# Low halves of the second product's activations on VectorE, and another order of its seven partial products

## The chip, the cores and the metric

The kernel runs on one core of a Trainium2 chip. The metric is device time in microseconds (us) for one execution; a median of several runs stands for a kernel. The engines of the core work side by side, each through its own queue in order: TensorE (PE in the profile; its weight loads are PEld), VectorE (DVE), ScalarE (ACT), GpSimd (POOL) and SyncE (SP), which here only issues transfers. They wait for each other by semaphores.

## The reference

One layer of a decoder: a combined input projection, two mixers (a gated recurrence and a short convolution), an output projection, and a dense MLP with a squared ReLU, each followed by a layer norm. There are 2048 prompt tokens and 64 sample tokens; the model width is 1024, the MLP's inner width 4096, all in float32.

```python
    mix = jnp.einsum('btm,md->btd', jnp.concatenate([o.astype(x.dtype), yc], axis=-1), w_out)
    x = _layer_norm(ALPHA * x + mix, ln1_g, ln1_b)

    hid = jnp.square(jax.nn.relu(jnp.einsum('btd,df->btf', x, w_ff1)))
    x = _layer_norm(ALPHA * x + jnp.einsum('btf,fd->btd', hid, w_ff2), ln2_g, ln2_b)
```

The change lies in the product of `hid` with `w_ff2`.

## The kernel before

The prompt is cut into four blocks (`b` = 0 to 3) of 512 tokens. Each block goes through the mixers and the output projection (`main` and the loops behind it), the MLP's first product (`ff1`) and its second (the loop over `pl["ff2"]`). The 64 sample tokens go with block 1 (`samp`).

**Three matmuls for one.** A float32 operand is split into a high part that TensorE takes in its fp32r form and a low part, the rest. `mm3_on` (L234 to L238) makes high x high (L236), high x low weights (L237) and low x high weights (L238). `h` and `l` are the parts of the activations, `wh` and `wl` of the weights. A high part is a copy on ScalarE, a low part a subtraction.

**Weights.** A weight unit is 128 x 1024 values. `unit_dma` (L173) has SyncE load it into one of three buffers `st`; `unit_split` makes `wh` on ScalarE (L194) and `wl` on VectorE (L201), four buffers each. `weights(u)` keeps this up to three units ahead of the matmuls. The subtraction isn't issued at once: it goes to the list `later`, and `flush` issues what the list holds at the start of the next `weights` call. `split` (L154 to L156) is the same for any tile: a copy on ScalarE at once, the subtraction on VectorE by way of `later`.

**Seven products for eight.** The second product is done in eight chunks `c` of 512 inner values, each as a 2 x 2 block product in seven multiplications. The activations of a chunk are the tile `raw[c]` with four slots (two halves of the inner values times two halves of the tokens). The weights are quarters (`B11`, `B21`, `B12`, `B22`) or sums of quarters (`T1` to `T4`), which GpSimd's accumulating transfers write to DRAM during block 0 (`make_sums`, called from block 0's `main` loop). `PRODUCTS` sets the order of the seven steps and the pair of PSUM banks (`A` to `D`) into which a step adds; inside a step all chunks follow each other. `INTO` says where a step's banks are added to the output rows once its last chunk is done: `add_to`, on VectorE (L1069, L1072), reads the bank from PSUM, first the bank of the first 128 tokens (its six matmuls come first), then the other. Steps of one letter go on adding into the same banks. The last chunk of block 3 is done in plain form at the very end (`pl["last"]`), and its activations are split during the last step.

**Activations of a step.** `prepare` runs two units ahead of the matmuls. It copies slot `SLOT_OF[step]` of `raw[c]` to `h` on ScalarE (L1040) and has GpSimd subtract to get `l` (L1041). Three of the seven steps need a sum of slots that isn't in `raw` yet: after `T4`, `T2` and `T1` were prepared, a subtraction on VectorE writes the next one (L1045, L1047, L1049), by way of `later`, eight in each of these steps. One more sum is made while `ff1` runs (`chunk_done`, L990).

**Sample rows, block 1.** Four steps (`SAMPLE`) also multiply the sample tokens, both parts in one tile `hp` (`sample_rows`, `mm_pair`, L241 and L242): four matmuls after the unit's twelve. At the step's end `sample_sums` copies half of the bank to SBUF on ScalarE (`upper`, L247) and adds twice on VectorE for each half of the output that the step goes into (L1080 or L1083, then L1084): two operations for `B21`, `T1` and `B22`, four for `B11`.

**Next block's input.** `X_PLACES` says behind which units of the second product the next block's input tiles (`X`) are loaded and split, as units of their own in the same queue.

The lines that set the order:

```python
PRODUCTS = (("B21", "C"), ("B11", "A"), ("T4", "D"), ("T2", "A"), ("T1", "B"), ("B22", "B"), ("T3", "A"))
INTO = {"C": {"B21": ((2, 0, 1),)}, "D": {"T4": ((0, 0, 1),)},
        "A": {"B11": ((2, 0, 1),), "T2": ((2, 1, -1),), "T3": ((0, 1, -1), (0, 0, 1))},
        "B": {"T1": ((0, 1, -1),), "B22": ((2, 1, -1),)}}
```

Of the kernel before, what the change touches and what calls it, by code (L numbers as in the profile page):

```python
# [9 lines left out]
F32 = mybir.dt.float32  # L10
F32R = mybir.dt.float32r
U8 = mybir.dt.uint8
AF = mybir.ActivationFunctionType
ALU = mybir.AluOpType
# [3 lines left out]
D = 1024  # L18
# [17 lines left out]
RAW = {"B11": 0, "B21": 1, "B12": 2, "B22": 3}  # L36
SUMS = ("T1", "T2", "T3", "T4")

PRODUCTS = (("B21", "C"), ("B11", "A"), ("T4", "D"), ("T2", "A"), ("T1", "B"), ("B22", "B"), ("T3", "A"))

SLOT_OF = {"B21": 3, "B11": 1, "T4": 2, "T2": 2, "T1": 1, "B22": 3, "T3": 0}

# [3 lines left out]

SAMPLE = {"B21": (1, ((0, 1),)), "B11": (0, ((0, 1), (1, -1))), "T1": (0, ((1, 1),)), "B22": (1, ((1, 1),))}

X_PLACES = (("B21", 2), ("B21", 5), ("B11", 2), ("B11", 5), ("B22", 5))
M_ORDER = (4, 5, 6, 7, 0, 1, 2, 3)  # L50


# [1 line left out]
def hybrid_step(ctx, tc, a, o):  # L54
# [89 lines left out]
    later = []  # L144
# [9 lines left out]
    def split(hi, lo, src):  # L154
        s.activation(hi, src, AF.Copy)  # L155
        later.append(lambda: v.tensor_tensor(lo, src, hi.bitcast(F32), ALU.subtract))  # L156
# [5 lines left out]
    def add_unit(src, scale=None, cols=D, use=None, spare=False):  # L162
        units.append((src, scale, cols, use, spare))
        return len(units) - 1
# [12 lines left out]
    def unit_split():  # L177
        i = at["split"]
        at["split"] += 1
        _, scale, _, use, spare = units[i]  # L180
        st = stages.pop(i)
        if use is not None:
            use(st)
            return
        wh = new((P, D), "wh", 4, F32R)
        if i == 0:
            wl = new((P, D), "wl", 4, F32R)
            for half in (slice(0, D // 2), slice(D // 2, D)):
                split(wh[:, half], wl[:, half], st[:, half])
                flush()  # L190
            handles[i] = (wh, wl)
            return
        if scale is None:
            s.activation(wh, st, AF.Copy)  # L194
        else:
            s.activation(wh, st, AF.Identity, scale=scale)

        def low():
            wl = TOK(F32R) if spare else new((P, D), "wl", 4, F32R)
            if scale is None:  # L200
                v.tensor_tensor(wl, st, wh.bitcast(F32), ALU.subtract)  # L201
            else:
                v.scalar_tensor_tensor(wl, st, scale, wh.bitcast(F32), ALU.mult, ALU.subtract)
            handles[i] = (wh, wl)

        later.append(low)
# [10 lines left out]
    def weights(i, kept=0):  # L217

        ahead(i + 4 - kept)
        return handles.pop(i)  # L220
# [111 lines left out]
                yield  # L332

    making = make_sums()

    for b in range(NB):
        pl = {}
# [16 lines left out]
        nx = x_units(b + 1) if b + 1 < NB else []  # L354
        for step, _ in PRODUCTS:
            for c in range(pl["nc"]):
                pl["ff2"].append((step, c, add_unit(a["w_ff2"][c * 4 + RAW[step]] if step in RAW else sums[c][step])))
                if (step, c) in X_PLACES and nx:
                    src, cols, use = nx.pop(0)
                    add_unit(src, cols=cols, use=use)  # L360
# [11 lines left out]
    for b in range(NB):  # L372
# [451 lines left out]

        for i, _ in enumerate(main()):
            rec_step()
            if b == 0 and i >= 4:
                next(making, 0)
                next(making, 0)
            if i >= 16 and i % (3 if samp else 4) == 0:  # L830
                rec_step()
            if i % 2 == 0:
                pump()
# [199 lines left out]
        def prepare():  # L1033
            if not queue:
                return
            step, c = queue.pop(0)
            r = raw[c]
            x = r[:, SLOT_OF[step]]
            h, l = F((P, 2, 256), "h", 3, F32R), F((P, 2, 256), "l", 3, F32R)
            s.activation(h, x, AF.Copy)  # L1040
            g.tensor_tensor(l, x, h.bitcast(F32), ALU.subtract)  # L1041
            hid[step, c] = (h, l)

            if step == "T4":
                later.append(lambda: v.scalar_tensor_tensor(x, r[:, 0], -1.0, x, ALU.mult, ALU.subtract))  # L1045
            elif step == "T2":
                later.append(lambda: v.scalar_tensor_tensor(r[:, 1], x, -1.0, r[:, 1], ALU.mult, ALU.subtract))  # L1047
            elif step == "T1":
                later.append(lambda: v.scalar_tensor_tensor(r[:, 3], r[:, 2], -1.0, r[:, 3], ALU.mult, ALU.subtract))  # L1049
            elif step == "T3":  # L1050
                del raw[c]

        for i, (f, u) in enumerate(pl["ff1"]):
            if i >= len(pl["ff1"]) - 2:
                prepare()
            ff1(f, weights(u), segs)
        drain()
        norm_weights(1)
        if b == 0:
            for _ in making:  # L1060
                pass

        touched = set()

# [31 lines left out]
        to = dict(PRODUCTS)  # L1096
        banks = {}
        sample_rows()
        for step, c, u in pl["ff2"]:
            w = weights(u)  # L1100
            parts = [tuple(x[:, q * 512:q * 512 + 512] for x in w) for q in range(2)]
            prepare()
            if step in SAMPLE:
                sample_rows()
            if step == "T3" and pl["last"] and 2 <= c < 6:
                if c == 2:
                    last = [F((P, 4, 2, 256), "raw", NCH, F32R) for _ in range(2)]
                split(last[0][:, c - 2], last[1][:, c - 2], raw[NCH - 1][:, c - 2])
# [159 lines left out]
```

## Time and profile before

| what | value |
|---|---|
| median of 3 runs | 2449.08 us (2446.64 to 2449.68) |
| profiled execution, its own time | 2449.19 us |
| its span, first to last instruction | 2447.4 us |
| granted TensorE clock, mean | 0.996 |
| GpSimd, `l` (L1041) | 217 instructions, 391.6 us busy |
| VectorE, `wl` (L201) | 514 instructions, 679.5 us busy, 1325 ns mean |
| ScalarE, `h` (L1040) | 217 instructions, 133.5 us busy |

In a row of waits, "PE ps L238 <- POOL l L1041: 2.2, 4, 0.9" says that TensorE's instruction of L238, which writes `ps`, was idle 2.2 us in all, four times, 0.9 at the longest, until GpSimd's instruction of L1041 had written `l`. In the order of time a row gives start, duration, engine, line, operation, `out<-in`, size and, in brackets, the idle time before it and what ended it. Matmuls are pipelined, so their durations overlap. A row of windows gives the stretch, its length, and for PE, PEld, DVE, ACT and POOL the busy time with the number of instructions, then clock, share of the DMA engines and GB/s. A group's row ends in busy time, mean ns of one, idle time before and what ended it.

### The profile page before, as it was taken

To read this page: it belongs to the slowest core of one execution; us is meant where nothing else is said; L and a number is where in the kernel's file an instruction comes from. 1 tells how busy PE (TensorE), PEld (TensorE's weight loads), DVE (VectorE), ACT (ScalarE), POOL (GpSimd) and SP (SyncE) were. 2 spreads that over 40 slices of the span, in tenths; PEclk is the share of its full clock that TensorE was granted. 3 is DMA by queue.
4 is the path that set the end of the run, shared out by engine and by line. 5 is a ranking of instruction groups with operands and counts; after the bars stand their busy time and mean duration, and the time that the engine had idled before them with its cause. 6 is when DMAs were issued, how large, how long until landed. Compare 5 with 4: busy or idle time off the path is not lost. (4 is left out here: it accounts for less than half of the span.)

```text
span 2447.4 us, 32997 instructions
## 1 busy us (share of the span) xinstructions
PE 2400.3 (98%) x12876; PEld 2051.5 (84%) x12876; DVE 1542.2 (63%) x2153; ACT 1114.9 (46%) x1794; POOL 524.9 (21%) x376
## 2 busy tenths in 40 slices
PE   7999999999999999999999999999999999999998
PEld 5888988878889889998778888988878888988876
DVE  5756822696865684227968857623886865822597
ACT  4334534654324354445554244534654334543553
POOL 3210000654001110004750000001662001000554
PEclk9999999999999999999999999999999999999999
DMA  9985423655223633225543225423654324433453
GB/s 329 277 233 174 160 97 112 199 186 179 79 78 75 211 121 104 87 96 164 180 149 118 91 80 190 144 96 129 206 188 146 104 82 159 161 103 116 163 184 113
DMA packets 103548, 358.79 MB, mean 147 GB/s; under 512 B 11552, under 2 KB 16032, under 8 KB 103392
## 3 DMA queue, kind: packets, MB, share of 16 engines
q1 hardware_dynamic: 91216, 313.88, 38.6%
q0 software_dynamic: 12032, 42.54, 6.5%
q8 instruction: 101, 1.65, 0.3%
q14 instruction: 55, 0.45, 0.1%
q10 hardware_dynamic: 144, 0.26, 0.0%
HBM read 345.59 MB, written 44.60 MB: 159 GB/s over the span
## 5 line engine op out<-in xcount | busy, mean ns | idle before, releaser
L201 DVE TENSOR_TENSOR wl<-st,wh 128x1024 fp32r<-128x1024 f32 x514 | 679.5, 1325 | 548.3 <-ACT wh L194 547.5
L230 PE MATMUL ps<-X,wh 128*128 128x512 f32 (+2 forms) x2272 | 779.6, 343 | 14.2 <-ACT X L155 11.0
L232 PE MATMUL ps<-X,wl 128*128 128x512 f32 (+2 forms) x2272 | 769.4, 339 | 1.0 <-DVE wl L201 1.0
L231 PE MATMUL ps<-X,wh 128*128 128x512 f32 (+2 forms) x2272 | 769.4, 339 | 0.5 <-DVE X L156 0.5
L194 ACT ACTIVATE wh<-st 128x1024 fp32r<-128x1024 f32 x515 | 543.1, 1055 | 381.0 <-DMA st<-T 90.8
L1041 POOL TENSOR_TENSOR l<-raw,h 128x512 fp32r<-128x512 f32 x217 | 391.6, 1808 | 947.3 <-ACT h L1040 930.9
L230 PEld LDWEIGHTS ps<-X,wh 128*128 128x128 f32 x2272 | 431.6, 190 | 60.6 <-ACT X L155 13.0
L232 PEld LDWEIGHTS ps<-X,wl 128*128 128x128 f32 x2272 | 431.3, 190 | 43.7 <-DVE wl L201 1.9
L231 PEld LDWEIGHTS ps<-X,wh 128*128 128x128 f32 x2272 | 431.7, 190 | 42.1 <-DVE X L156 2.6
L238 PE MATMUL ps<-wh,l 128*128 128x512 f32 x868 | 342.1, 394 | 8.9 <-POOL l L1041 8.9
L236 PE MATMUL ps<-wh,h 128*128 128x512 f32 x868 | 339.1, 391 | 6.3 <-DVE tok L1072 5.0
L237 PE MATMUL ps<-wl,h 128*128 128x512 f32 x868 | 339.2, 391 | 1.6 <-DVE wl L201 1.6
L1008 ACT ACTIVATE raw<-ps 128x256 f32<-128x256 f32 (+1 forms) x184 | 85.7, 466 | 372.6 <-PE ps L232 370.9
L238 PEld LDWEIGHTS ps<-wh,l 128*128 128x128 f32 x868 | 163.3, 188 | 53.1 <-POOL l L1041 19.9
L236 PEld LDWEIGHTS ps<-wh,h 128*128 128x128 f32 x868 | 163.4, 188 | 40.7 <-issue 6.2
L237 PEld LDWEIGHTS ps<-wl,h 128*128 128x128 f32 x868 | 163.2, 188 | 37.4 <-DVE wl L201 3.3
L1040 ACT ACTIVATE h<-raw 128x512 fp32r<-128x512 f32 x217 | 133.5, 615 | 7.7 <-PE ps L237 5.7
L262 POOL TENSOR_TENSOR sm<-sm,nhalf 128x1 f32<-128x1 f32 (+1 forms) x34 | 36.5, 1075 | 383.4 <-DVE sm L261 383.4
L230 PE MATMUL ps<-wh,X 128*128 128x512 f32 x256 | 104.0, 406 | 0.0
L230 PE MATMUL ps<-wh,S 128*128 128x512 f32 x256 | 101.3, 396 | 0.0
L232 PE MATMUL ps<-wh,X 128*128 128x512 f32 x256 | 100.3, 392 | 0.0
L232 PE MATMUL ps<-wh,S 128*128 128x512 f32 x256 | 99.9, 390 | 0.0
(204 smaller groups left out, 2560.4 us busy)
## 6 DMA issues: line engine op xcount, KB each, us to landing
st<-in_w_ff SPq DMA_DIRECT2D x249, 512.0 KB, 3.3
st<-T SPq DMA_DIRECT2D x124, 512.0 KB, 3.3
st<-in_w_in SPq DMA_DIRECT2D x110, 512.0 KB, 3.3
st<-in_w_out SPq DMA_DIRECT2D x56, 512.0 KB, 4.3
T<-in_w_ff POOLq DMA_DIRECT2D x48, 512.0 KB, 19.7
T<-T POOLq DMA_DIRECT2D x16, 512.0 KB, 17.8
lnb<-in_lnb SPq DMA_DIRECT2D x16, 512.0 KB, 5.9
tok<-in_x SPq DMA_DIRECT2D x16, 512.0 KB, 6.9
```

Of the source, the lines that this page charges most:

```text
L194: s.activation(wh, st, AF.Copy)
L201: v.tensor_tensor(wl, st, wh.bitcast(F32), ALU.subtract)
L230: te.matmul(out, lh, rh, start=first, stop=False)
L231: te.matmul(out, lh, rl, start=False, stop=False)
L232: te.matmul(out, ll, rh, start=False, stop=last)
L236: te.matmul(out, lh, rh, start=first, stop=False, skip_group_check=True)
L237: te.matmul(out, lh, rl, start=False, stop=False, skip_group_check=True)
L238: te.matmul(out, ll, rh, start=False, stop=last, skip_group_check=True)
L262: g.tensor_tensor(st[:n, 15:16], st[:n, 14:15], nhalf[:n, 0:1], ALU.pow)
L1008: s.activation(r[:, h0:h1], ps[:, :256 * (h1 - h0)].rearrange("p (s t) -> p s t", t=256), AF.Relu)
L1040: s.activation(h, x, AF.Copy)
L1041: g.tensor_tensor(l, x, h.bitcast(F32), ALU.subtract)
```

## The change

`l` is now made by `split`: the subtraction goes to VectorE, by way of `later`. `PRODUCTS` has another order: `T4`, `B11`, `B21`, `T2`, `T1`, `T3`, `B22`. The three kinds of sums are no longer tied to `prepare`: `sum_rows` puts one into `later` every one and a half units, number s (from 0) at unit (3s + 6) // 2, so that 24 of them (21 in block 3) lie in the first five steps. The input tiles of the next block are loaded in the last two steps instead of the first two (and one in the sixth). `make_sums` is stepped from the ninth part of `main` instead of the fifth, and its rest, if any, is issued ahead of the first product's main loop. Where the last chunk is split moves with the last step, to `B22`.

```diff
-PRODUCTS = (("B21", "C"), ("B11", "A"), ("T4", "D"), ("T2", "A"), ("T1", "B"), ("B22", "B"), ("T3", "A"))
+PRODUCTS = (("T4", "D"), ("B11", "A"), ("B21", "C"), ("T2", "A"), ("T1", "B"), ("T3", "A"), ("B22", "B"))
...
-X_PLACES = (("B21", 2), ("B21", 5), ("B11", 2), ("B11", 5), ("B22", 5))
+X_PLACES = (("T3", 0), ("T3", 4), ("B22", 0), ("B22", 3), ("B22", 5))
...
-            if b == 0 and i >= 4:
+            if b == 0 and i >= 8:
                 next(making, 0)
                 next(making, 0)
...
-            s.activation(h, x, AF.Copy)
-            g.tensor_tensor(l, x, h.bitcast(F32), ALU.subtract)
+            split(h, l, x)
             hid[step, c] = (h, l)
-
-            if step == "T4":
-                later.append(lambda: v.scalar_tensor_tensor(x, r[:, 0], -1.0, x, ALU.mult, ALU.subtract))
-            elif step == "T2":
-                later.append(lambda: v.scalar_tensor_tensor(r[:, 1], x, -1.0, r[:, 1], ALU.mult, ALU.subtract))
-            elif step == "T1":
-                later.append(lambda: v.scalar_tensor_tensor(r[:, 3], r[:, 2], -1.0, r[:, 3], ALU.mult, ALU.subtract))
-            elif step == "T3":
+            if step in ("T2", "T1", "B22"):
+                assert (step, c) in summed
+            seen.add((step, c))
+            if step == "B22":
                 del raw[c]
 
+
+        sumq = [(k, c) for k in ("T2", "T1", "B22") for c in range(ncs)]
+        summed, seen = set(), set()
+
+        def sum_rows():
+            if not sumq:
+                return
+            k, c = sumq.pop(0)
+            assert (dict(T2="T4", T1="B11", B22="B21")[k], c) in seen
+            summed.add((k, c))
+            r = raw[c]
+            to, of, less = {"T2": (2, 0, 2), "T1": (1, 2, 1), "B22": (3, 2, 3)}[k]
+            later.append(lambda: v.scalar_tensor_tensor(r[:, to], r[:, of], -1.0, r[:, less], ALU.mult, ALU.subtract))
+
+        if b == 0:
+            for _ in making:
+                pass
         for i, (f, u) in enumerate(pl["ff1"]):
...
         drain()
         norm_weights(1)
-        if b == 0:
-            for _ in making:
-                pass
...
-        for step, c, u in pl["ff2"]:
+        for n_, (step, c, u) in enumerate(pl["ff2"]):
             w = weights(u)
+            while (len(summed) * 3 + 6) // 2 <= n_ and sumq:
+                sum_rows()
             parts = [tuple(x[:, q * 512:q * 512 + 512] for x in w) for q in range(2)]
             prepare()
...
-            if step == "T3" and pl["last"] and 2 <= c < 6:
+            if step == "B22" and pl["last"] and 2 <= c < 6:
```

What this does to the queues is shown at three places. VectorE in block 0, at the end of a step behind which a sum stands: `T4` before the change (the two `tok` rows are its adds from the banks).

```order
L201 TENSOR_TENSOR wl_4087<-st_4067,wh_4069 128x1024
L1047 SCALAR_TENSOR_TENSOR raw_2149<-raw_2149 128x512
L1072 SCALAR_TENSOR_TENSOR tok_1776<-tok_1776,ps_3935 128x512
L1072 SCALAR_TENSOR_TENSOR tok_1778<-tok_1778,ps_3936 128x512
L201 TENSOR_TENSOR wl_4112<-st_4090,wh_4092 128x1024
L1047 SCALAR_TENSOR_TENSOR raw_2311<-raw_2311 128x512
```

The same engine with the change, at the end of `B11` in block 0.

```order
L1084 SCALAR_TENSOR_TENSOR tok_1929<-tok_1929,ps_3736 128x512
L1084 SCALAR_TENSOR_TENSOR tok_1931<-tok_1931,ps_3737 128x512
L201 TENSOR_TENSOR wl_3910<-st_3889,wh_3891 128x1024
L1063 SCALAR_TENSOR_TENSOR raw_2149<-raw_2149 128x512
L156 TENSOR_TENSOR l_3894<-raw_2311,h_3893 128x512
L201 TENSOR_TENSOR wl_3935<-st_3914,wh_3916 128x1024
```

Before, no `l` stood in this queue; now each unit has one, behind the unit's `wl` and sum, and all three behind the adds.

TensorE in block 0, where `T1` ends, before: its last three matmuls and the first three of `B22` (`ps_4309` and `ps_4310` are the pair B).

```order
L236 MATMUL ps_4310<-wh_4397,h_4422 128x512
L237 MATMUL ps_4310<-wl_4415,h_4422 128x512
L238 MATMUL ps_4310<-wh_4397,l_4423 128x512
L236 MATMUL ps_4309<-wh_4420,h_4445 128x512
L237 MATMUL ps_4309<-wl_4438,h_4445 128x512
L238 MATMUL ps_4309<-wh_4420,l_4446 128x512
```

With the change `T3` follows, into the pair A (`ps_3736` and `ps_3737`; B is `ps_4290` and `ps_4291`).

```order
L236 MATMUL ps_4291<-wh_4377,h_4402 128x512
L237 MATMUL ps_4291<-wl_4394,h_4402 128x512
L238 MATMUL ps_4291<-wh_4377,l_4403 128x512
L236 MATMUL ps_3736<-wh_4400,h_4428 128x512
L237 MATMUL ps_3736<-wl_4417,h_4428 128x512
L238 MATMUL ps_3736<-wh_4400,l_4429 128x512
```

The bank that VectorE has to read at the end of `T1` was written again by the next matmul, and is now left alone for a step.

VectorE in block 1, between two steps that both have sample rows. Before, from `B21` to `B11` (`tok_7428` holds the sample rows, `ps_9836` their bank):

```order
L1072 SCALAR_TENSOR_TENSOR tok_7424<-tok_7424,ps_9822 128x512
L1072 SCALAR_TENSOR_TENSOR tok_7426<-tok_7426,ps_9823 128x512
L1083 SCALAR_TENSOR_TENSOR tok_7428<-tok_7428,ps_9836 64x512
L1084 TENSOR_TENSOR tok_7428<-tok_7428,h_10055 64x512
L201 TENSOR_TENSOR wl_10059<-st_10027,wh_10029 128x1024
L156 TENSOR_TENSOR hp_10035<-tok_7678,hp_10035 128x2x64
```

With the change, from `B11` to `B21`:

```order
L1084 SCALAR_TENSOR_TENSOR tok_7424<-tok_7424,ps_10002 128x512
L1084 SCALAR_TENSOR_TENSOR tok_7426<-tok_7426,ps_10003 128x512
L1095 SCALAR_TENSOR_TENSOR tok_7428<-tok_7428,ps_10016 64x512
L1096 TENSOR_TENSOR tok_7428<-tok_7428,h_10230 64x512
L1095 SCALAR_TENSOR_TENSOR tok_7428<-tok_7428,ps_10016 64x512
L1096 TENSOR_TENSOR tok_7428<-tok_7428,h_10230 64x512
L201 TENSOR_TENSOR wl_10236<-st_10203,wh_10205 128x1024
L1063 SCALAR_TENSOR_TENSOR raw_7690<-raw_7690 128x512
L156 TENSOR_TENSOR l_10208<-raw_7860,h_10207 128x512
L156 TENSOR_TENSOR hp_10210<-tok_7678,hp_10210 128x2x64
```

The `hp` that the next unit's sample rows need now stands behind four additions of sample rows instead of two, and behind a sum and an `l`.

More of the change, by code (lines that the diff above doesn't have):

```diff
@@ L179, in unit_split @@
         at["split"] += 1
-        _, scale, _, use, spare = units[i]
+        src, scale, _, use, spare = units[i]
         st = stages.pop(i)
@@ L334, in hybrid_step, with quarter2 @@
     making = make_sums()
+    def quarter2(c, k):
+        return a["w_ff2"][c * 4 + RAW[k]] if k in RAW else sums[c][k]
     for b in range(NB):
@@ L356, in hybrid_step @@
             for c in range(pl["nc"]):
-                pl["ff2"].append((step, c, add_unit(a["w_ff2"][c * 4 + RAW[step]] if step in RAW else sums[c][step])))
+                pl["ff2"].append((step, c, add_unit(quarter2(c, step))))
                 if (step, c) in X_PLACES and nx:
```

## The prediction

> **What bounds the kernel now.** I read the page's busy times first, then the second product's four stretches by windows, then TensorE's waits inside each, and last the order of time around the longest waits.
>
> ```profile
> PE 2400.3 (98%) x12876; PEld 2051.5 (84%) x12876; DVE 1542.2 (63%) x2153; ACT 1114.9 (46%) x1794; POOL 524.9 (21%) x376
> ```
>
> TensorE is the bound: only its gaps can be won. The second product runs in four stretches, one for each block of tokens (windows; span, then the busy time of each engine):
>
> ```profile
> 433.80:593.00 159.20, 155.49 (x675) 125.14 (x675) 127.29 (x100) 93.78 (x120) 92.64 (x54) 1.00 0.62 200
> 1097.30:1289.00 191.70, 185.17 (x804) 148.96 (x803) 149.14 (x139) 102.31 (x156) 109.18 (x54) 1.00 0.50 164
> 1701.20:1862.30 161.10, 154.76 (x675) 125.74 (x675) 125.06 (x97) 92.57 (x117) 97.62 (x54) 1.00 0.60 196
> 2274.40:2414.10 139.70, 136.39 (x592) 111.25 (x591) 108.44 (x87) 79.70 (x103) 81.83 (x47) 0.99 0.55 181
> ```
>
> The pace comes from a part without waits, the last 16 units of the first block (a unit is one step and chunk, 12 matmuls):
>
> ```profile
> 549.16 0.47 PE L236 MATMUL ps<-wh,h 128*128 128x512 f32 x1 [1.15 <-DVE tok L1072]
> ...
> 592.56 0.39 PE L238 MATMUL ps<-wh,l 128*128 128x512 f32 x1
> ```
>
> 191 steps in 43.40 us are 0.227 us each, 2.72 us a unit. A unit with sample rows has four more matmuls, 3.63 us. Each matmul is shown 0.39 us long, so a wait costs the idle time shown and 0.16 more. TensorE's waits in the four windows, in their order:
>
> ```profile
> PE ps L238 <- POOL l L1041: 2.2, 4, 0.9
> PE ps L236 <- DVE tok L1072: 1.1, 1, 1.1
> PE ps L237 <- DVE wl L201: 0.4, 1, 0.4
> ...
> PE ps L241 <- DVE hp L156: 3.1, 3, 1.3
> PE ps L238 <- POOL l L1041: 2.2, 2, 1.4
> PE ps L237 <- DVE wl L201: 1.2, 1, 1.2
> ...
> PE ps L238 <- POOL l L1041: 3.8, 4, 1.4
> PE ps L236 <- ACT h L1040: 1.3, 1, 1.3
> PE ps L236 <- DVE tok L1072: 1.2, 1, 1.2
> ...
> PE ps L236 <- DVE tok L1072: 2.6, 1, 2.6
> PE ps L238 <- POOL l L1041: 0.7, 1, 0.7
> ```
>
> By block: 3.7, 6.5, 6.3 and 3.3 us idle in 6, 6, 6 and 2 waits. With 0.16 each that is 4.7, 7.5, 7.3 and 3.6. The wait of 2.6 costs more behind it:
>
> ```profile
> 2374.80 0.55 PE L236 MATMUL ps<-wh,h 128*128 128x512 f32 x1
> ...
> 2378.14 0.47 PE L238 MATMUL ps<-wh,l 128*128 128x512 f32 x1
> ```
>
> Eight steps take 3.34 us instead of 1.82: 1.5 us at a slower pace. So these waits can give back 4.7 + 7.5 + 7.3 + 5.1 = **24.6 us**. The first stretch is 159.2 - 675 x 0.227 = 6.0 us longer than its matmuls; what is not in the 4.7 is in pieces too small for the list of waits, and I leave it as it is.
>
> **Why TensorE waits there.** VectorE and GpSimd hold each other up (order of time, first block):
>
> ```profile
> 537.01 0.68 DVE L1049 SCALAR_TENSOR_TENSOR raw<-raw 128x512 f32<-128x512 f32 x1
> 537.61 1.21 DVE L201 TENSOR_TENSOR wl<-st,wh 128x1024 fp32r<-128x1024 f32 x1
> 537.62 2.34 POOL L1041 TENSOR_TENSOR l<-raw,h 128x512 fp32r<-128x512 f32 x1 [1.61 <-ACT h L1040]
> 538.75 1.76 DVE L1049 SCALAR_TENSOR_TENSOR raw<-raw 128x512 f32<-128x512 f32 x1
> 540.30 1.35 POOL L1041 TENSOR_TENSOR l<-raw,h 128x512 fp32r<-128x512 f32 x1 [0.34 <-ACT h L1040]
> 540.43 2.31 DVE L201 TENSOR_TENSOR wl<-st,wh 128x1024 fp32r<-128x1024 f32 x1
> ```
>
> Whichever starts second is long: wl takes 1.21 us when it is first and 2.31 when l stands before it; l takes 1.35 first and 2.34 second; the sum 0.68 or 1.76. So the two stand in line: 1.21 + 1.35 = 2.56 of a unit's 2.72 us, before any sum, and a sum of 0.68 in the same unit makes 3.24. That is why l, wl and what is queued behind them come late. The groups of the first window (mean ns behind the comma), and of the first product before it, where an operation of l's shape and types stands:
>
> ```profile
> L201 DVE TENSOR_TENSOR wl<-st,wh 128x1024 fp32r<-128x1024 f32 x55 | 88.7, 1620 | 22.4 <-ACT wh L194 22.3
> ...
> L156 DVE TENSOR_TENSOR X<-h,X 128x512 fp32r<-128x512 f32 x4 | 2.7, 684 | 0.0
> ```
>
> **The change: l on VectorE.** 54 instructions of GpSimd go from the first window and 54 come on VectorE, of the shape of the X row: 54 x 0.684 = 36.9 us. wl falls from a mean of 1.62 to 1.21, 55 x 0.41 = 22.6 us less. With sums at 0.68 (24 x 0.68 = 16.3), 14 adds at 0.69 (9.7) and five x loads of wl's size (6.1), VectorE needs 66.6 + 36.9 + 16.3 + 9.7 + 6.1 = 135.6 us, each counted in full. TensorE's own time is 56 x 2.72 = 152.3. VectorE fits, at 89%, and the waits for l on GpSimd and for wl go. So does the one for h in block 2, which stood among them in T1's pass (1.3 and 0.16 us; if it stays, that is its price), and the three for hp in block 1, whose successors I work out below. I cost GpSimd's idle time at nothing: in the other stretches it waits for VectorE as before.
>
> **The order of products.** T1 and B22 both add into bank B, and stood side by side: TensorE had to let VectorE read the bank first (the three tok waits). Now T3 lies between, 8 units or 21.8 us, and these waits and the 1.5 us go entirely.
>
> **What is late next: l behind the adds.** At the end of a product VectorE reads two banks, and what it does next stands behind that (end of B22, first block):
>
> ```profile
> 569.87 0.69 DVE L1069 TENSOR_TENSOR tok<-tok,ps 128x512 f32<-128x512 f32 x1 [1.34 <-PE ps L238]
> ...
> 571.02 0.39 PE L236 MATMUL ps<-wh,h 128*128 128x512 f32 x1
> ...
> 571.22 0.69 DVE L1069 TENSOR_TENSOR tok<-tok,ps 128x512 f32<-128x512 f32 x1 [0.67 <-PE ps L238]
> ```
>
> Count from the next unit's first matmul (571.02). The second add starts at 0.20. A 512-wide operation lets the next start 0.60 later (537.01 to 537.61), wl 1.14 later (537.61 to 538.75). So wl starts at 0.80, a sum at 1.94, l at 2.54; l ends at 3.22 and TensorE can use it 0.05 later, 3.27. The unit after next wants it at its third matmul, 2.72 + 0.45 = 3.17: a wait of 0.1. A sum stands there at three ends of a block (T4, B11, T2): 0.3 us. T3 has four adds and no sum: 0.20 + 3 x 0.60 = 2.00, wl 2.00, l 3.14 to 3.82, wait 0.7. So 1.0 us in each of blocks 0, 2 and 3.
>
> **The x loads** move from passes one and two to six and seven, four within 12 units before and now (five in block 0). Two waits for l in block 0 and one in block 2 stand in the units right behind them now:
>
> ```profile
> 470.18 0.50 PE L238 MATMUL ps<-wh,l 128*128 128x512 f32 x1 [0.36 <-POOL l L1041]
> ...
> 479.29 0.50 PE L238 MATMUL ps<-wh,l 128*128 128x512 f32 x1 [0.65 <-POOL l L1041]
> ...
> 1746.05 0.50 PE L238 MATMUL ps<-wh,l 128*128 128x512 f32 x1 [0.68 <-POOL l L1041]
> ```
>
> There h and l stood behind an x that waited for its load. Nothing shortens the loads, so I keep it: 1.3 us in block 0, 0.8 in block 2. Bounds: nothing, or 1.6 us (the longest l wait, 1.4, and 0.16) at each of 13 loads, 21 us; I stay with the rows.
>
> **Block 1, the sample rows.** Now B11 and B21 are neighbours there, both with sample rows; B21 and B11 were before, which shows the price:
>
> ```profile
> 1126.18 0.39 PE L242 MATMUL ps<-wl,hp 128*128 128x512 f32 x1
> ...
> 1127.30 0.68 DVE L1083 SCALAR_TENSOR_TENSOR tok<-tok,ps 64x512 f32<-64x512 f32 x1 [0.91 <-ACT h L247]
> 1128.01 0.68 DVE L1084 TENSOR_TENSOR tok<-tok,h 64x512 f32<-64x512 f32 x1
> 1128.62 1.21 DVE L201 TENSOR_TENSOR wl<-st,wh 128x1024 fp32r<-128x1024 f32 x1
> 1129.76 0.28 DVE L156 TENSOR_TENSOR hp<-tok,hp 128x128 fp32r<-128x128 f32 x1
> ...
> 1130.18 0.47 PE L241 MATMUL ps<-wh,hp 128*128 128x512 f32 x1 [0.89 <-DVE hp L156]
> ```
>
> The next unit starts at 1126.18 + 0.23 = 1126.41 and wants hp at 2.72; it came at 3.77: 1.05 lost. The sums of B11 are four instead of two (0.60 + 0.71 more), and a sum and an l (0.60 each) now stand before hp. That is 1.05 + 2.51 = 3.56 us at one place, 3.4 idle. It is longer than the 2.6 that slowed the pace, so I add 1.5. The Trainium skill, "TensorE: Matmul & The Clock Gate", What's actually happening, says that the clock falls after an idle window of about 3.4 us that runs freely. By that the 2.6 us could have cost nothing behind it; the trace shows 1.5, so the row decides. By the page the sum could end 1.5 us lower.
>
> Behind B21 and behind T1 two sums of samples are followed by short units: wl at 2.21, l at 3.35 to 4.03, usable at 4.08 for 3.17: 0.9 each. Block 1 keeps 3.56 + 1.5 + 1.8 = 6.9 us of its 7.5.
>
> **Edits at nothing.** GpSimd's rows up to the first l, the sums of weights among them, are the same before and now, with the same waits for each other; the later start moves text only. The x loads go through the same queue of SyncE and the same three buffers, and their number is the same. The 24 sums are the same arithmetic, one and a half units apart. The part for the last chunk stays in the last pass.
>
> **The sum.** Left: 1.0 + 1.3 in block 0, 6.9, 1.0 + 0.8, and 1.0, that is 12.0. Won: 24.6 - 12.0 = **12.6 us**. The profiled execution took 2449.19 (span 2447.4), 0.1 above the median of 2449.08, so 2449.2 - 12.6 = **2436.6**.
>
> **Rivals.** (1) *VectorE becomes the bound; slower.* If its long durations in these stretches are not GpSimd's doing, they stay, and l has them too: 54 x 0.684 x 1.62 / 1.21 = 49 us beside the 127.3 in the first window make 176 for 159.2, 17 too many. In the same way the others have 6, 13 and 12 too many (47 l's in the last): 48 us, about 2497. It decides from a mean wl of 1.51 (135.6 + 55 x 0.30 = 152). The 1.21 and 2.31 within 3 us of each other speak against it. The Trainium skill, "Perfetto Trace Analysis", Optimizing Scalar/DVE Operations, is on its side: work is to be taken off a saturated VectorE, if need be to GpSimd, and this change does the reverse; the same place warns that the two share a read port. (2) *The waits only change their names.* If each of six product ends costs the 0.7 of T3's, that is 4.2 in each of blocks 0, 2 and 3 instead of 1.0: 9.6 more, 2446.2. VectorE's 89% leaves little to catch up with. (3) *Nearly all waits go:* the x loads and hp cost nothing and ends stay at 1.0: 24.6 - 3.0, 2427.6. For it: l's way gets shorter, 0.68 us instead of 1.8. Against: hp's queue is in the order itself. That the change doesn't do what it says can be left out: no l stands on GpSimd any more.
>
> **How the numbers follow.** The forecast has 0.60, rival 3 0.15, rival 2 0.17, rival 1 0.06, and 0.02 are for what I don't see. From 2427 to 2447 holds eight in ten. This kernel's runs tell 0.2%, 4.9 us, from no change; faster is below 2444.2: 0.60 + 0.15 and 0.07 of rival 2, so 0.82; the same 0.12; slower 0.06.
>
> **What would show it.** Right: GpSimd is hardly busy in the four stretches (381 us in the windows now); wl has its 1.21 us in them; no wait for tok at a B22; short waits for l two units after product ends; one wait for hp of over 3 us in block 1 with a slow pace behind it. Wrong: a mean wl above 1.5 us, or VectorE without gaps between units while TensorE waits.

## The result and the profile after

The changed kernel takes **2431.02 us**, the median of four runs (2430.45 to 2433.41), beside 2448.94 for the kernel before in the same session (2446.64 to 2449.68): a ratio of 0.9930, 95% interval 0.9913 to 0.9947. That is 17.9 us less; the forecast was 12.6 less. The profiled execution took 2430.45, its span 2428.6.

The page of the changed kernel, busy times first, then the rows of `wl` and `l` (busy, mean ns of one, idle time before):

```profile
PE 2393.4 (99%) x12876; PEld 2050.9 (84%) x12876; DVE 1535.9 (63%) x2370; ACT 1115.1 (46%) x1794; POOL 132.4 (5%) x159
...
L201 DVE TENSOR_TENSOR wl<-st,wh 128x1024 fp32r<-128x1024 f32 x514 | 627.8, 1222 | 500.6 <-ACT wh L194 499.8
...
L156 DVE TENSOR_TENSOR l<-raw,h 128x512 fp32r<-128x512 f32 x217 | 148.5, 684 | 30.1 <-ACT h L155 30.1
```

GpSimd's 392 us of `l` are gone. VectorE makes 217 more instructions, 148.5 us of them, and is still busy for 6.3 us less in all (1542.2 before): `wl` fell from 1325 to 1222 ns on the mean, the 93 sums from 126.7 us in all to 63.6, and `hp` from 27.9 to 9.1. What GpSimd gave away cost VectorE nothing, because VectorE had been paying for it (pool_reads, below, brings this back).

The changed kernel's four stretches of the second product, in the columns used before:

```profile
433.00:587.80 154.80, 154.38 (x677) 125.96 (x676) 126.61 (x154) 93.11 (x118) 0.00 (x0) 1.00 0.63 199
1090.50:1279.20 188.70, 184.17 (x800) 150.29 (x799) 139.04 (x193) 101.26 (x154) 0.00 (x0) 0.99 0.51 166
1692.20:1848.40 156.20, 154.85 (x676) 125.88 (x675) 126.88 (x153) 92.82 (x116) 0.00 (x0) 1.00 0.63 199
2260.50:2395.70 135.20, 134.66 (x592) 110.34 (x591) 110.27 (x136) 79.70 (x103) 0.00 (x0) 1.00 0.59 187
```

From the first matmul of a stretch to the end of its last one of L236 to L238, the lengths are these. With `B22` last, block 1 ends in four sample matmuls that fall outside this count; 4 x 0.227 = 0.9 is added there for the kernels marked *.

| us | block 0 | 1 | 2 | 3 | sum |
|---|---|---|---|---|---|
| before | 159.1 | 191.5 | 161.0 | 139.5 | 651.1 |
| changed * | 154.6 | 189.4 | 156.0 | 135.0 | 635.0 |
| l_only | 153.0 | 188.2 | 153.5 | 133.4 | 628.1 |
| order_only * | 154.8 | 192.9 | 156.8 | 133.5 | 638.0 |
| order_tied * | 157.3 | 193.1 | 159.5 | 134.5 | 644.4 |
| t3_moved * | 159.7 | 191.2 | 159.1 | 136.2 | 646.1 |
| t3_last | 153.5 | 190.2 | 154.8 | 134.2 | 632.7 |

So 16.1 of the span's 18.8 us come from these stretches. TensorE's waits over the whole span of the changed kernel (us in all, times, longest) hold no `tok` any more, and the `l` of GpSimd is replaced by a quarter as much for the `l` of VectorE (8.9 in 11 waits before):

```profile
PE ps L241 <- DVE hp L156: 3.3, 1, 3.3
...
PE ps L238 <- DVE l L156: 2.3, 4, 0.7
...
PE ps L237 <- DVE wl L201: 0.6, 3, 0.3
```

### The profile page after: what moved, and what is told of

Read it like the earlier page. It is cut to its first block, busy times and chain, and to the rows that moved or that the text cites. A ratio compares the mean times of both kernels' runs of the same rounds, so it can differ in the third digit from the quotient of the medians.

```text
span 2428.6 us, 32948 instructions
## 1 busy us (share of the span) xinstructions
PE 2393.4 (99%) x12876; PEld 2050.9 (84%) x12876; DVE 1535.9 (63%) x2370; ACT 1115.1 (46%) x1794; POOL 132.4 (5%) x159
## 4 chain that ended last, share of the span: by engine, by line
PE 49%; DVE 2%; DMA 1%; issue 0%; ACT 0%; ACTq 0%; DVEq 0%; SPq 0%
PE ps L230 11%; PE ps L232 10%; PE ps L231 10%; PE ps L238 5%; PE ps L236 5%; PE ps L237 5%; PE ps L654 1%; DMA st<-T 1%; DVE wl L201 1%; PE ps L241 0%; PE ps L242 0%; DMA st<-in_w_ff 0%; DVE tok L1081 0%; PE ps L743 0%; PE ps L740 0%
## 5 line engine op out<-in xcount | busy, mean ns | idle before, releaser
L201 DVE TENSOR_TENSOR wl<-st,wh 128x1024 fp32r<-128x1024 f32 x514 | 627.8, 1222 | 500.6 <-ACT wh L194 499.8
L230 PE MATMUL ps<-X,wh 128*128 128x512 f32 (+2 forms) x2272 | 778.2, 343 | 15.7 <-ACT X L155 12.4
L230 PEld LDWEIGHTS ps<-X,wh 128*128 128x128 f32 x2272 | 430.5, 189 | 61.3 <-ACT X L155 14.0
L238 PE MATMUL ps<-wh,l 128*128 128x512 f32 x868 | 340.3, 392 | 2.8 <-DVE l L156 2.3
L236 PE MATMUL ps<-wh,h 128*128 128x512 f32 x868 | 338.3, 390 | 0.0
L238 PEld LDWEIGHTS ps<-wh,l 128*128 128x128 f32 x868 | 163.1, 188 | 43.9 <-DVE l L156 10.5
L236 PEld LDWEIGHTS ps<-wh,h 128*128 128x128 f32 x868 | 163.2, 188 | 33.3 <-ACT h L155 0.3
L156 DVE TENSOR_TENSOR l<-raw,h 128x512 fp32r<-128x512 f32 x217 | 148.5, 684 | 30.1 <-ACT h L155 30.1
L155 ACT ACTIVATE h<-raw 128x512 fp32r<-128x512 f32 x217 | 133.5, 615 | 3.7 <-PE ps L237 2.2
L230 PE MATMUL ps<-wh,X 128*128 128x512 f32 x256 | 104.0, 406 | 0.0
L230 PE MATMUL ps<-wh,S 128*128 128x512 f32 x256 | 101.3, 396 | 0.0
```

Source lines behind the costliest of these rows:

```text
L230: te.matmul(out, lh, rh, start=first, stop=False)
L236: te.matmul(out, lh, rh, start=first, stop=False, skip_group_check=True)
L238: te.matmul(out, ll, rh, start=False, stop=last, skip_group_check=True)
```

## The experiments

Two theories at first. **T**: all of it comes from taking `l` off GpSimd, which ends the standing in line; the order adds little. **R1**: about half comes from the order of products and the spread sums. A second question is whether the line itself cost time, or GpSimd's long way to an `l` (R2).

### The two halves of the change, alone

l_only, the kernel before with

```diff
-            s.activation(h, x, AF.Copy)
-            g.tensor_tensor(l, x, h.bitcast(F32), ALU.subtract)
+            split(h, l, x)
```

> The kernel before with one edit: l goes to VectorE by way of later; order of products, sums and input loads stay as before. Theory T (the gain comes from ending the standing in line of VectorE and GpSimd; the waits for tok at T1 to B22 came only from VectorE being late, so the order adds little): wl falls to 1.21 us in the four stretches, the waits for tok are gone or under 1 us in all, time 2431 us, from 2428 to 2435. Rival R1 (about half of the 18 us comes from the order of products and the spread sums): the waits for tok at T1 to B22 stay, 3 to 5 us in all, time about 2440, from 2437 to 2444.

order_only, the changed kernel with the same lines the other way round:

```diff
-            split(h, l, x)
+            s.activation(h, x, AF.Copy)
+            g.tensor_tensor(l, x, h.bitcast(F32), ALU.subtract)
```

> The changed kernel with one edit: l is back on GpSimd; order of products, spread sums and late input loads are those of the change. T: wl stays at 1.6 us and the waits for l on GpSimd stay; only the waits for tok (5 us idle and 1.5 us of slow pace) may go, and hp at B11 to B21 adds some: 2444 to 2455. R1: about 2440, from 2437 to 2444.

Measured in one session: l_only **2427.02** us (2424.90 to 2428.73), ratio 0.9913 (0.9899 to 0.9928); order_only **2432.14** (2428.14 to 2434.77), ratio 0.9933 (0.9918 to 0.9948). Either half alone brings nearly the whole gain, 20.9 and 15.7 us by the medians against 17.9 for both. T is right on the first (and even there the time is a little under its range) and fell on the second; R1 fell on both. The halves don't add, they are two cures for one trouble. And the whole change is not better than its first half alone. order_only has more in it than the places of the steps: the spread sums, the late input loads and the later `make_sums`. The last shows nothing ahead of the second product, which starts at 432.2 to 434.1 us in the kernels with the old start of `make_sums` and at 432.2 to 434.4 in those with the new one.

In l_only TensorE's waits in block 1 are most of what is left of the 19.8 us idle in the second product before; in blocks 0, 2 and 3 there are 0.2 us, 0.6 and none. Block 1 of l_only:

```profile
PE ps L241 <- DVE hp L156: 2.9, 2, 1.4
PE ps L238 <- DVE l L156: 2.7, 2, 2.0
```

No wait for `tok` is among them, though `T1` and `B22` are neighbours in this kernel and share their bank. So those waits, 5.0 us before, came from VectorE being late, not from the bank alone. In order_only the long durations are still there (page of order_only):

```profile
L201 DVE TENSOR_TENSOR wl<-st,wh 128x1024 fp32r<-128x1024 f32 x514 | 699.2, 1367 | 525.7 <-ACT wh L194 524.8
```

with a mean `wl` of 1367 ns, above the 1325 before, and yet the waits for `l` fell from 8.9 to 4.7 us. The line was there and cost less. Which part of the order did that is taken up below.

### Is it the line, or the way by GpSimd?

pool_reads, the changed kernel with an operation of GpSimd that nobody waits for, one for each unit:

```diff
             split(h, l, x)
+            g.tensor_tensor(idle, x, h.bitcast(F32), ALU.subtract)
```

> The changed kernel, and GpSimd makes for each unit a subtraction with the operands and types of the old l into a tile that nothing reads; no other engine waits for it. T (it is the two engines' standing in line that costs): wl goes back to a mean above 1.6 us, l and the sums are lengthened as well; a unit then needs 1.21 + 1.35 and l's own 0.68 or more, over 3.2 us of its 2.72, so that VectorE is late in each unit: 0.5 us or more in each of 217 units, over 2500 us. Rival R2 (it was the long way by way of GpSimd, 1.35 to 2.34 us for l, that made l late; the lengthening of wl cost nothing): about 2431, up to 2436.

pool_writes, the changed kernel with a fill instead, of the same size and as often, ahead of VectorE's `l`:

```diff
+            g.memset(l.bitcast(F32), 0.0)
             split(h, l, x)
```

> The changed kernel, and GpSimd fills the tile of each l with zeros before VectorE writes l into it: GpSimd writes as much as it did, but reads nothing. If the two engines stand in line for their reads alone: wl stays at 1.21 us, and the time is 2431 us, up to 2436. If any work of GpSimd on SBUF holds VectorE up: wl rises above 1.4 us and the time goes above 2445, toward that of the kernel in which GpSimd reads too.

pool_reads takes **2535.96** us (2533.72 to 2537.01), ratio 1.0358 (1.0342 to 1.0373): 105 us more than the changed kernel. pool_writes takes **2430.69** (2428.95 to 2432.08), ratio 0.9929 (0.9912 to 0.9946), the changed kernel's time. T's time holds, and R2's falls; the mean `wl` is 1311 ns (1409 in block 0), not the 1600 that T expected, because the lengthening falls on `l` and the sums as well. Two units of pool_reads in the order of time on VectorE (start, duration):

```profile
499.86 1.21 DVE L201 TENSOR_TENSOR wl<-st,wh 128x1024 fp32r<-128x1024 f32 x1
501.00 1.78 DVE L1065 SCALAR_TENSOR_TENSOR raw<-raw 128x512 f32<-128x512 f32 x1
502.70 0.68 DVE L156 TENSOR_TENSOR l<-raw,h 128x512 fp32r<-128x512 f32 x1
503.30 1.21 DVE L201 TENSOR_TENSOR wl<-st,wh 128x1024 fp32r<-128x1024 f32 x1
504.44 1.78 DVE L156 TENSOR_TENSOR l<-raw,h 128x512 fp32r<-128x512 f32 x1
506.14 1.21 DVE L201 TENSOR_TENSOR wl<-st,wh 128x1024 fp32r<-128x1024 f32 x1
```

and on GpSimd:

```profile
500.88 1.35 POOL L1044 TENSOR_TENSOR tok<-raw,h 128x512 f32<-128x512 f32 x1 [1.50 <-ACT h L155]
504.31 1.35 POOL L1044 TENSOR_TENSOR tok<-raw,h 128x512 f32<-128x512 f32 x1 [2.09 <-ACT h L155]
```

In these rows an unused subtraction makes the VectorE operation that starts just behind it 1.10 us longer (1.78 for 0.68). It started 0.12 ahead, so it keeps VectorE out for 1.22 us. A unit of VectorE's work takes 3.44 us with a sum and 2.84 without, where TensorE wants one each 2.72: VectorE sets the pace. TensorE's stretch in block 0 is 185.5 us. The sum from the rows says so too: 24 units of 3.44 and 32 of 2.84 are 173.4, and five input loads of 1.14 and fourteen adds of 0.60 bring it to 187.5. In pool_writes a fill and `wl` overlap and nothing changes, on GpSimd and then on VectorE:

```profile
500.95 0.53 POOL L1043 MEMSET l<- 128x512 f32 x1 [2.19 <-PE ps L238]
```

```profile
500.55 1.22 DVE L201 TENSOR_TENSOR wl<-st,wh 128x1024 fp32r<-128x1024 f32 x1
501.68 0.68 DVE L1064 SCALAR_TENSOR_TENSOR raw<-raw 128x512 f32<-128x512 f32 x1
```

It is what GpSimd reads that stands in VectorE's way here, not what it writes. The Trainium skill, "SBUF — State Buffer", Who interferes with whom, has this rule: an instruction of VectorE with two inputs in SBUF contends with one of GpSimd that reads SBUF, and not with one that only writes. The two runs agree. In pool_reads VectorE makes `l` as well, which it did not in the kernel before. So the run shows that standing in line costs time, but not how much of the 8.9 us of waits for `l` before was the line and how much the 1.35 us that GpSimd takes for an `l` even when nothing holds it up. That split stays open.

### Why the order alone cured it too

Theory A: with `l` on GpSimd a unit costs the pair 1.14 + 1.22 = 2.36 us, and 0.60 more with a sum: 2.96. Tied to three steps, eight such units in a row fall 8 x 0.24 = 1.9 us behind TensorE's 2.72, right ahead of the two adds at the step's end; spread over two units in three, the mean is 2.76, about TensorE's pace. (An estimate, from the rows above.) Theory B: it is the bank, free for a step longer.

order_tied, order_only with the sums tied again:

```diff
+            elif step in ("T4", "T2", "T1"):
+                sum_rows()
...
-            while (len(summed) * 3 + 6) // 2 <= n_ and sumq:
-                sum_rows()
```

> The changed kernel with two edits: l is back on GpSimd, and the sums are tied to prepare again, one behind each unit of T4, T2 and T1, as before; the order of products and the late input loads stay as changed. Theory A (with l on GpSimd it is the bunching of the sums that makes VectorE late: eight units of 1.21 + 1.35 + 0.68 = 3.24 us against 2.72, so spreading the sums was what the new order's 16 us came from): the waits for l and wl come back in and behind those steps, 2440 to 2449 us. Theory B (it was the free bank between T1 and B22): as with spread sums, 2430 to 2435 us.

t3_moved, the kernel before with the place of `T3` alone changed:

```diff
-("T1", "B"), ("B22", "B"), ("T3", "A"))
+("T1", "B"), ("T3", "A"), ("B22", "B"))
```

> The kernel before with one edit: T3 stands between T1 and B22 (and the fifth input load of the first seven steps, as well as the split for the last chunk, keep their places by moving to the other step's name); l stays on GpSimd, the sums stay tied. By the prediction's step on the order (the bank that VectorE reads at the end of T1 is free for eight units more): the three waits for tok and the slow pace in block 3 go, 5.0 us idle, 0.5 us around them and 1.5 us of slow pace, 7 us in all, less what T3's four adds cost now that a step stands behind them, 0.7 to 1.2 us in four blocks: 2443 to 2447. If VectorE's lateness only moves to the next wait, for l or wl: within 2 us of 2448.6.

order_tied: **2444.46** us (ten runs, 2442.18 to 2448.65), ratio 0.9986 (0.9976 to 0.9996). A's range is met and B's is not: bunched again, the sums cost 12.3 us by the medians of two sessions. How much of order_only's gain that is stays open. In the stretches of the two profiles 6.4 of its 13.1 us are gone, about half, and TensorE's waits for `l` and `wl`, which A expected back, only grow from 6.5 to 7.8 us; those for `hp` in block 1 grow from 3.9 to 6.3. (`T4` is the first step here, so two of its sums fall into the first product; the time between the stretches is the same as before, so that cost TensorE nothing.) What the late loads and the order of the first three steps do with `l` on GpSimd was not run alone. t3_moved: **2443.60** (ten runs, 2441.41 to 2449.11), ratio 0.9987 (0.9977 to 0.9996). The free bank by itself is worth a few microseconds. It does take the waits for `tok` away, all three, but the waits for GpSimd's `l` grow from 8.9 to 12.0 us (t3_moved):

```profile
PE ps L238 <- POOL l L1041: 12.0, 13, 1.4
```

In block 0 the stretch even gets 0.6 us longer: TensorE no longer stops for the bank, and stops for the late `l` instead. In block 3, where the wait had also slowed the pace, 3.3 us are won.

### What the order costs once VectorE is on time

l_only beats the changed kernel by 6.9 us in the four stretches, and by 4.0 at the medians; 1.5 us of the difference is lost outside them, as the last section tells. Three runs take the rest of the change apart. sums_tied, the changed kernel with the diff of order_tied above:

> The changed kernel with one edit: the sums are tied to prepare again, one behind each unit of T4, T2 and T1; l stays on VectorE. Theory A: a unit with a sum needs 1.21 + 0.68 + 0.68 = 2.57 us of VectorE's 2.72, so nothing comes late inside a step and the time stays within 2 us of 2431. If spreading counts with l on VectorE too: slower by the 4 us or more that the eight units of a step pile up, 2435 or more.

x_early, the changed kernel with

```diff
-X_PLACES = (("T3", 0), ("T3", 4), ("B22", 0), ("B22", 3), ("B22", 5))
+X_PLACES = (("T4", 2), ("T4", 5), ("B11", 2), ("B11", 5), ("B22", 5))
```

> The changed kernel with one edit: the next block's input tiles are loaded in the first two steps again, as before the change. If the late loads cost what stands behind them in the trace of the changed kernel (0.3 us in block 0, 0.4 in block 1, 0.6 in block 2): 2429 to 2431 us, and those waits gone. If the loads delay l wherever they stand (my prediction's 1.3 and 0.8 us): 2431 us, with the waits at the new places.

t3_last, the changed kernel with

```diff
-("T1", "B"), ("T3", "A"), ("B22", "B"))
+("T1", "B"), ("B22", "B"), ("T3", "A"))
```

> The changed kernel with one edit: B22 and T3 change places, so that T3 is last as before the change (late input loads and the split of the last chunk keep their units). If T3's place costs, with l on VectorE, what stands behind T3's end in the trace of the changed kernel (waits for wl and l in the ninth unit behind T3's start, 0.7 us in blocks 0, 2 and 3, 0.8 in block 1), and the bank of T1 and B22 costs nothing because VectorE is on time: 2427 to 2429 us, no wait for tok at B22. If the bank costs as it did before the change: the waits for tok are back, 2433 us or more.

sums_tied: **2429.38** (2428.23 to 2430.16), ratio 0.9927 (0.9912 to 0.9942), as A expects; its stretches are 3.2 us shorter than the changed kernel's. Bunching does no harm when VectorE has room. What helps a little is the place in the queue: `sum_rows` puts a sum ahead of `l`, the tied form behind it. Behind the adds of `T4` in block 0, VectorE of the changed kernel runs

```profile
455.04 0.69 DVE L1084 SCALAR_TENSOR_TENSOR tok<-tok,ps 128x512 f32<-128x512 f32 x1 [0.67 <-PE ps L238]
455.64 1.22 DVE L201 TENSOR_TENSOR wl<-st,wh 128x1024 fp32r<-128x1024 f32 x1
456.78 0.69 DVE L1063 SCALAR_TENSOR_TENSOR raw<-raw 128x512 f32<-128x512 f32 x1
457.38 0.69 DVE L156 TENSOR_TENSOR l<-raw,h 128x512 fp32r<-128x512 f32 x1
```

and TensorE's third matmul of the unit, which needs this `l`, starts 0.05 after it ends:

```profile
457.79 0.39 PE L237 MATMUL ps<-wl,h 128*128 128x512 f32 x1
458.12 0.50 PE L238 MATMUL ps<-wh,l 128*128 128x512 f32 x1
458.46 0.39 PE L236 MATMUL ps<-wh,h 128*128 128x512 f32 x1
```

This is a wait that no list of waits shows: the row has no idle time in brackets, since the matmul ahead is drawn 0.39 long. Its start is 0.33 behind the last one instead of 0.227, and the next start 0.34 behind it again: 0.22 us lost.

x_early: **2432.57** (2430.63 to 2434.47), ratio 0.9941 (0.9926 to 0.9955). The late loads cost no more than the early ones, rather less: early, block 0 is 1.6 us longer and block 1 0.7 by the stretches. Both expectations, at 2431 or below, are missed by 1.6 us at the median, and the second is nearer. The waits behind the late loads do go, but others come at the early places: they stand behind the loads wherever these are, and there are more of them early (block 0 of x_early, where the changed kernel has one wait of 0.2 in its list):

```profile
PE ps L238 <- DVE l L156: 2.0, 5, 0.5
```

t3_last: **2431.42** (2430.01 to 2432.56), ratio 0.9931 (0.9917 to 0.9946), against an expectation of 2427 to 2429: missed. What stood behind T3's end did go (1.1, 1.2 and 0.8 us in blocks 0, 2 and 3), and no wait for `tok` came back, so the bank costs nothing while VectorE is on time. But in block 1 `T1` and `B22`, which both have sample rows, are neighbours again, and a second wait for `hp` appears there (t3_last), which the expectation had left out:

```profile
1230.54 0.47 PE L241 MATMUL ps<-wh,hp 128*128 128x512 f32 x1 [1.43 <-DVE hp L156]
```

The stretches are 2.4 us shorter in all; 1.5 us of that is lost again outside them, in a place told of in the last section.

### The wait for hp, and the queue's own order

hp_now, the changed kernel with one line behind the split of `hp`:

```diff
                 split(hp[:, :, 0:NS], hp[:, :, NS:P], rs[f // 16][:, f % 16:f % 16 + 2, :])
+                later.pop()()
```

> The changed kernel with one edit: the low part of hp is issued at once instead of by way of later, so that it stands ahead of wl, the sum and l on VectorE. If hp is late because of what stands ahead of it in the queue: the wait of 3.3 us and the slow pace of 1.5 us behind it go; the l of that unit, which comes 4 us or more after the step's end too, then shows a wait of its own, up to 2 us: 2426 to 2429 us. If the slow pace has another cause it stays: 1.5 us more.

In the changed kernel the step from `B11` to `B21` in block 1 ran so, on VectorE:

```profile
1143.52 0.67 DVE L1095 SCALAR_TENSOR_TENSOR tok<-tok,ps 64x512 f32<-64x512 f32 x1
1144.22 0.68 DVE L1096 TENSOR_TENSOR tok<-tok,h 64x512 f32<-64x512 f32 x1
1144.83 1.21 DVE L201 TENSOR_TENSOR wl<-st,wh 128x1024 fp32r<-128x1024 f32 x1
1145.97 0.68 DVE L1063 SCALAR_TENSOR_TENSOR raw<-raw 128x512 f32<-128x512 f32 x1
1146.57 0.67 DVE L156 TENSOR_TENSOR l<-raw,h 128x512 fp32r<-128x512 f32 x1
1147.17 0.28 DVE L156 TENSOR_TENSOR hp<-tok,hp 128x128 fp32r<-128x128 f32 x1
```

and on TensorE, where the starts behind the wait are 0.43 apart:

```profile
1147.59 0.77 PE L241 MATMUL ps<-wh,hp 128*128 128x512 f32 x1 [3.35 <-DVE hp L156]
1148.16 0.63 PE L242 MATMUL ps<-wl,hp 128*128 128x512 f32 x1
1148.58 0.63 PE L241 MATMUL ps<-wh,hp 128*128 128x512 f32 x1
```

hp_now takes **2428.65** us (2427.90 to 2429.77), ratio 0.9925 (0.9910 to 0.9940), inside its expectation. The wait and the slow pace are gone together, so the pace was the wait's doing. The `l` that stood ahead of `hp` now shows its own lateness, as expected (hp_now):

```profile
1148.74 0.50 PE L238 MATMUL ps<-wh,l 128*128 128x512 f32 x1 [1.70 <-DVE l L156]
```

Block 1 gains 3.6 us. From this and l_only followed two attempts at a better kernel. l_only_first, l_only with

```diff
             split(h, l, x)
+            later.insert(0, later.pop())
```

> The kernel l_only (l on VectorE in the old order) with one edit more: l stands ahead of wl and of a sum in later. If what is left there is l behind wl: the waits for l at the ends of steps go (0.3 us in block 0, 2.2 and 0.8 in block 1, 0.8 in block 2), the two waits for hp of 1.6 us in block 1 stay or grow by 0.6 each; 2423 to 2425 us. If wl is then late instead: 2427 us.

l_only_both, l_only_first with the line of hp_now:

> The kernel l_only_first, and the low part of hp is issued at once as in hp_now. If each of TensorE's waits left in the second product is a matter of the place in VectorE's queue: nearly no wait is left in the four stretches, 7 us less than l_only, 2419 to 2422 us. If VectorE is too full there for any order of its queue: a wait for wl or for tok takes their place, 2424 us or more.

l_only_first: **2433.84** (2433.34 to 2435.45), ratio 0.9943 (0.9928 to 0.9958). l_only_both: **2430.10** (2428.44 to 2431.02), ratio 0.9926 (0.9911 to 0.9940). The times hoped for are both missed: in block 1 the edits do what they were made for (186.1 and 183.5 us for l_only's 188.2), but block 0 gets 5.1 and 6.5 us longer and block 2 4.3 and 3.4. l_only_both falls under its second expectation, 2424 or more with a wait for `wl`, though not because VectorE is full (block 0 of l_only_both):

```profile
PE ps L236 <- ACT h L155: 1.8, 3, 0.9
PE ps L237 <- DVE wl L201: 1.3, 1, 1.3
```

VectorE of l_only_first in block 0:

```profile
471.21 0.69 DVE L156 TENSOR_TENSOR l<-raw,h 128x512 fp32r<-128x512 f32 x1 [1.06 <-ACT h L155]
471.82 1.22 DVE L156 TENSOR_TENSOR X<-st,X 128x1024 fp32r<-128x1024 f32 x1
473.63 0.69 DVE L156 TENSOR_TENSOR l<-raw,h 128x512 fp32r<-128x512 f32 x1 [0.60 <-ACT h L155]
```

and ScalarE there:

```profile
469.59 1.06 ACT L155 ACTIVATE X<-st 128x1024 fp32r<-128x1024 f32 x1 [0.71 <-DMA st<-in_xt]
470.56 0.62 ACT L155 ACTIVATE h<-raw 128x512 fp32r<-128x512 f32 x1
```

`h` stands on ScalarE behind the input tile that waits for its load; `l`, now first, waits for `h`, and all that is ready stands behind it. Block 3, in which no input is loaded, takes 133.4 us in l_only and in both of these, and in blocks 0 and 2 all that l_only_first loses lies in the first 18 units, where the loads are. The old place of `l`, behind work whose inputs come earlier, was the better one where inputs are late. The lowest median is that of l_only, but its runs overlap those of hp_now; hp_now's line on l_only, without the move of `l`, was not tried.

## Why the prediction held, and where it was off

**l on VectorE: right.** `l` takes 684 ns and `wl` 1222 in the stretches, as costed, and VectorE fits: 126.6 us of block 0's 154.8, for the 135.6 that counted each duration in full. pool_reads brings the standing in line back, and the lost time with it. The prediction's 2.56 and 3.24 us for a unit of the two in line add durations that overlap their neighbours; from start to start, as under theory A, they are 2.36 and 2.96.

**The order of products: right in what it does, not in why that counts.** The waits for `tok` went. But l_only and t3_last have none either with the bank shared, so with `l` on VectorE this step brought nothing of its own. The prediction's sum survived because it took each wait away once, whichever edit did it; that is luck.

**Edits at nothing: right here, for a reason it didn't have.** Spreading the sums was costed at nothing as "the same arithmetic". With `l` on GpSimd it was half of the order's gain or more (order_tied). It counted little only because the other half of the change had already taken the load off, and then it cost 3.2 us in the stretches (sums_tied).

**Late work behind the ends: right.** The end of `T4` in block 0 shows the prediction's places to a hundredth: counted from the add's start, `wl` at 0.60, the sum at 1.74, `l` at 2.34, which with its 0.20 are 0.80, 1.94 and 2.54. `hp` at `B11` to `B21` lost 3.50 us and 1.5 of slow pace, for 3.56 and 1.5. Behind `B21` and `T1` `l` and `wl` lost 0.83 each time, for 0.9; behind `T3` 0.7, for 0.7. The predicted idle of 0.1 at ends with a sum was real too and cost 0.22 each, as shown above.

**The loads of x: right in sum, by luck.** 1.3 us were kept in block 0, and 0.3 was lost near them there, in a step that no list of waits shows. In block 2 it was 0.8, and 1.4 were lost in two waits, both behind a weight unit that had waited for its own load (ScalarE idle for 1.57 and 1.47 us, with `h` queued behind the copy). Block 1, where nothing was kept, lost 0.4. So 2.1 us were lost for 2.1 predicted, but not where the prediction put them. With the loads early (x_early) none of these four is left in the last two steps, so they do come from the loads, though in block 2 by way of a late weight unit and not, as predicted, of an `h` behind an `x`.

**The term that was mis-sized** is "with 0.16 each", and with it the pieces "too small for the list of waits, and I leave it as it is". A wait costs its idle time, 0.16, and about 0.1 in the step behind it, and waits below 0.16 are in no list. By the stretches' lengths less 0.227 a matmul, TensorE lost 31.0 us before (6.6, 9.9, 8.5 and 6.0), where the prediction priced 24.6. The waits in the lists lost what they were priced at; some 2 of the other 6.4 us are the steps behind these 20 waits, and the rest is in pieces that no list shows. After, it is 14.9 (2.1, 7.8, 3.5 and 1.5) for a predicted 12.0. The parts left out shrank with the rest, from 6.4 to 2.9. The profiled spans differ by 18.8 us, 6.2 more than forecast, and 3.5 of these are that term. The others are outside the stretches: 0.8 in the first 433 us, where both kernels run the same instructions and the profiles of all runs spread from 432.2 to 434.4; 1.5 ahead of block 1's second product, below; and 0.5 behind the last stretch, where a wait for `wl` went.

**The rivals.** VectorE did not become the bound; pool_reads shows what that looks like, at 2536. The waits did change their names (`hp`, `l`, `wl` of VectorE), at half the price. "Nearly all waits go" is what l_only comes nearest to, without the half of the change that was to help it.

## What to carry to other kernels

When a change carries two edits against one wait, run each alone: here either gave nearly all, and the one that changed most of the code was not needed. Before an operation is moved from a slow engine to a busier one, see whether the two lengthen each other: moving 37 us of work to VectorE in block 0 left its busy time as it was. And an operation goes to the front of an engine's queue only if its inputs are there before those of the work it overtakes.

## What the hardware showed

Behind the same wait for the input of `L230`, 1.67 us in the kernel before and 1.66 in the changed one, with 0.26 and 0.27 at the next matmul, the granted clock (third column from the right) fell in one profile and not in the other. The kernel before:

```profile
911.00:915.00 4.00, 2.06 (x12) 1.63 (x11) 3.78 (x9) 2.38 (x7) 0.00 (x0) 0.87 0.46 146
915.00:920.00 5.00, 5.00 (x28) 5.00 (x28) 2.36 (x4) 0.67 (x3) 0.00 (x0) 0.76 0.00 0
```

and the changed one:

```profile
906.00:910.00 4.00, 2.08 (x14) 1.65 (x13) 3.77 (x9) 2.02 (x6) 0.00 (x0) 1.00 0.42 131
910.00:914.00 4.00, 4.00 (x29) 4.00 (x29) 1.99 (x3) 1.41 (x5) 0.00 (x0) 1.00 0.00 0
```

This is the 1.5 us. The stretch around it has one of two lengths in all profiles taken, 502.9 to 503.0 or 504.4 to 504.6. Seven profiles have the long one and a fallen clock at this place: the kernel before, l_only, l_only_first, order_tied, sums_tied, x_early and t3_last. In the other seven the wait is the same and the clock stays at 1.00. Whether a kernel always falls on the same side was not tried. The Trainium skill, "TensorE: Matmul & The Clock Gate", What's actually happening, says that the window in which idleness is judged runs freely; two outcomes of one wait agree with that, while its length of some 3.4 us doesn't show here, where 1.9 us in all were enough.
